# Block sums of a weight matrix and residual additions as accumulating transfers from GpSimd

## The chip, the cores and the metric

The kernel runs on one core of a Trainium2 chip. The metric is the device time of one execution in microseconds; lower is better. The engines are TensorE (PE, with its weight loads PEld), VectorE (DVE), ScalarE (ACT), GpSimd (POOL) and SyncE (SP), which issues the transfers.

## The reference

Two layers work on 256 tokens of width 1024. Each layer is a SwiGLU FFN (inner width 2816), a token mixer (a Mamba-2 branch and a gated DeltaNet branch), and a second FFN. The part that the change touches is the FFN:

```python
def swiglu(x, w_in, w_out):
    gate, up = jnp.split(x @ w_in, 2, axis=-1)
    return (jax.nn.silu(gate) * up) @ w_out

for l in range(DEPTH):
    h = h + 0.5 * swiglu(rms_norm(h, ffn1_norm[l]), ffn1_w_in[l], ffn1_w_out[l])
    ...   # the mixer adds to h
    h = h + 0.5 * swiglu(rms_norm(h, ffn2_norm[l]), ffn2_w_in[l], ffn2_w_out[l])
return rms_norm(h, final_norm)
```

All tensors are float32.

## The kernel before

Weights come from HBM in tiles of 128 x 1024 float32 (512 KB). Each form of a tile that TensorE uses is split into a high part (`whi`, a copy to float32r on ScalarE, line 67) and a low part (`wlo`, the difference on VectorE, line 70), and each product is three matmuls: high by high, low by high, high by low. A raw tile lives in a ring of NRAW = 5 buffers (`wraw`), and a split form in a ring of NSPL = 5 (`whi`, `wlo`). A load is issued by SP in order, and waits until the ring's oldest tile is done with, as a rule until its low part was computed.

An FFN of the kernel is written as a string, `FFN`: "f" is the first 256 inner channels, each "c" a chunk of 128 inner channels of gate and up (two weight tiles, 48 matmuls of 256 columns, into `fc`), and "A", "B", "d" are parts of the second product, `@ w_out`. The inner width is 22 blocks of 128. Six of them ("d") are multiplied directly. The other 16 are taken as eight pairs, two pairs to a group, so there are four groups in each of the four FFNs. For a pair the product is one of 2 x 2 blocks (two token halves, two inner blocks, two output halves) with seven block products in place of eight, each of sums of blocks. "A" runs four of the seven for a group of two pairs (into the PSUM tiles `p`), and "B" the other three (into `o`), after all chunks are done:

```python
FFN = "f" + 8 * "c" + "A" + 4 * "c" + "A" + 4 * "c" + "A" + 2 * "c" + "A" + 2 * "c" + "BdBBBddddd"
```

The sums of weight blocks are made on VectorE from the raw tiles of a group. `plan` lists the forms in the order of use, q0 to q3 for "A" and q4 to q6 for "B"; `prep` makes one form; `load` issues the load of one tile of `stream`; `take` hands a form to TensorE and keeps loads and forms ahead. The first tile of a group lies in a buffer of its own (`wfirst`, one of four slots that the mixer also uses), since its sum is kept from q0 to q6. Four sums a group are formed (`less`): three into `wfirst`, one into a `wraw` tile. Five tiles are loaded for a group: three at "A", and two at "B".

When all four "A" are done, `join` combines the four PSUM tiles with the factor 0.5 into the four quarters of the residual `h` (tiles `half`, `u2`, `u4`, `u5`; four additions to h). The products in `o` are added afterwards by `residual`, inside `norm_in`, where the next norm begins: square on ScalarE, `zz` on VectorE, the power -1/2 on GpSimd (`rsqrt`, line 190), the scaled rows `hn` on VectorE, and their transposes `hnT` on TensorE. The last part of an FFN, "ddddd", takes all five direct forms at once, for the first token half and then for the second.

The order on each engine comes from a scheduler that places an instruction when what it needs is there; a load whose buffer is free is put early. So the `wfirst` loads of an FFN stand on SP in the stage before it, where the slots come free.

Of the kernel before, what the change touches and what calls it, by code (L numbers as in the profile page):

```python
# [7 lines left out]
F32 = mybir.dt.float32  # L8
# [3 lines left out]
ALU = mybir.AluOpType  # L12
# [4 lines left out]
P = 128  # L17
# [6 lines left out]
FC = FF // 256  # L24
# [5 lines left out]
NRAW = 5  # L30
NSPL = 5
# [21 lines left out]
def trunk_kernel(ctx, tc, x, wst, wsm, norms, lpar, rpar, cst, out):  # L53
    nc = tc.nc
# [14 lines left out]
    def tt(o, a, b, op):  # L69
        return V.tensor_tensor(out=o, in0=a, in1=b, op=op)  # L70

    def stt(o, a, s, b, op0, op1):
        return V.scalar_tensor_tensor(out=o, in0=a, scalar=s, in1=b, op0=op0, op1=op1)  # L73
# [25 lines left out]

    def plan_plain(j, n):  # L100
        for i in range(j, j + n):
            stream.append(i)
            plan.append(("d", [len(stream) - 1], len(stream)))
        return j + n

    def plan_ffn(j):


        o, j2, held = j + 4 * FC, j + 4 * FC + 22, []
        for kind in FFN:  # L110
            if kind in "fc":
                j = plan_plain(j, 4 if kind == "f" else 2)
            elif kind == "d":
                o = plan_plain(o, 1)
            else:
                if kind == "A":
                    where = [len(stream) + i for i in range(3)]
                    stream.extend(range(o, o + 3))
                    held.append((where, o + 2))
                    o += 4  # L120
                    for i, need in enumerate((2, 3, 3, 3)):
                        plan.append((f"q{i}", where, where[0] + need))
                else:
                    where, b22 = held.pop(0)
                    where += [len(stream) + 1, len(stream)]
                    stream.extend([b22, b22 + 1])
                    for i in range(4, 7):
                        plan.append((f"q{i}", where, len(stream)))
        return j2

    j0 = 0
# [1 line left out]
        j0 = plan_ffn(plan_plain(plan_ffn(j0), mix))  # L133
    assert j0 == n_dram
    n_raw = len(stream)
    first = {js[0] for kind, js, _ in plan if kind == "q0"}
    n_forms = len(plan)
    state = {"loaded": 0, "prepped": 0, "taken": 0, "last": None, "hold": False, "behind": {}, "first": 0}
    raws, halves = {}, {}

    def load(j):
        if j in first:
            r = slots.tile([P, 1024], F32, tag=f"y{state['first']}", name="wfirst")
# [3 lines left out]
        state["last"] = nc.sync.dma_start(r[:], wst[stream[j] // 2, :, (stream[j] % 2) * 1024 :][:, 0:1024])  # L147
        raws[j] = r

    def prep(i):  # L150
        kind, js, _ = plan[i]
        hi = wpool.tile([P, 1024], F32R, tag="whi", name="whi", bufs=NSPL)
        lo = wpool.tile([P, 1024], F32R, tag="wlo", name="wlo", bufs=NSPL)

        def less(o, a, b):
            tt(raws[js[o]][:], raws[js[a]][:], raws[js[b]][:], ALU.subtract)


        r = raws[js[{"q2": 1, "q4": 4, "q5": 3}.get(kind, 0)]]
        with ExitStack() as behind:  # L160
            for ins in state["behind"].pop(i, ()):
                behind.enter_context(tc.issue_after(ins))
            act(hi[:], r[:])
            if kind == "q1":
                less(1, 2, 1)
            elif kind == "q2":
                less(0, 2, 0)
            elif kind == "q4":
                less(0, 3, 0)
            tt(lo[:], r[:], f(hi[:]), ALU.subtract)  # L170
            if kind == "q0":
                less(0, 1, 0)
        for o in {"d": (0,), "q2": (1,), "q3": (2,), "q4": (4,), "q5": (3,), "q6": (0,)}.get(kind, ()):
            raws.pop(js[o])
        halves[i] = (hi, lo)

    def ahead(key, n, fn):
        while state[key] < n:
            fn(state[key])
            state[key] += 1  # L180

    def take():
        j = state["taken"]
        state["taken"] = j + 1
        ahead("loaded", min(plan[min(j + NSPL, n_forms) - 1][2] + NRAW - 1, n_raw), load)
        ahead("prepped", min(j + 1 if state["hold"] else j + NSPL, n_forms), prep)
        return halves.pop(j)

# [204 lines left out]
    def join(pb):  # L393

        hv = [[h[:, t, n * 512 : (n + 1) * 512] for n in range(2)] for t in range(2)]
        half, u2, u4, u5 = (tmp2(n) for n in ("half", "u2", "u4", "u5"))
# [12 lines left out]
    def close_blocks(po, stat, sums, pb, nw):  # L409
# [24 lines left out]
    def ffn(nxt):  # L434
# [19 lines left out]
        def block_sums(p, g2):  # L454

            sf = tmp2("sf")
            a11, a21, a12, a22 = (g2[:, j * P : (j + 1) * P] for j in range(4))
            s1, s2_, s3, s4 = (sf[:, j * P : (j + 1) * P] for j in range(4))
            tt(s1, a21, a22, ALU.add)
            tt(s3, a11, a21, ALU.subtract)  # L460
            tt(s2_, s1, a11, ALU.subtract)
            tt(s4, a12, s2_, ALU.subtract)
# [27 lines left out]
        for c in range(FC - 1):  # L490
# [17 lines left out]
                block_sums(c + 1, g2)  # L508
            if todo[0] == "A":
                if not pb:  # L510
                    pb.update({i: trb(f"p{i}") for i in (1, 6, 5, 7)})
                four = [
                    (pb[1], lambda p: stat(2 * p, 0), PAIRS[n]),
                    (pb[5], lambda p: sums(p, 0), PAIRS[n]),
                    (pb[7], lambda p: sums(p, 2), PAIRS[n]),
                    (pb[6], lambda p: sums(p, 1), PAIRS[n]),
                ]
# [703 lines left out]
    for t in range(2):  # L1221
# [5 lines left out]
        r = rstd_of(t)  # L1227
# [137 lines left out]
```

## Time and profile before

| | |
|---|---|
| Median of 3 runs | 1567.72 us (1565.7 to 1568.12) |
| The profiled execution | 1568.61 us, span 1566.8 us |
| Granted TensorE clock | 0.999 |
| Transfers | 293.14 MB, mean 187 GB/s |
| `wraw` loads | 504 of 512 KB, 4.7 us from issue to landing |
| `wfirst` loads | 16 of 512 KB, 5.4 us from issue to landing |

A row of the profile's groups reads: line, engine, operation, written tile <- read tiles, shapes, count | busy us in total, mean ns of one | idle time of the engine just before, and what ended it. A row of waits reads: who waited, for whom, total us, times, longest us. A row of a timeline reads: start, duration, engine, line, operation, tiles, count, and in brackets the idle time before it. The share of the queue `q1` is the time that its packets took, of sixteen engines over the span.

### The profile page before, as it was taken

To read this page: it belongs to the slowest core of one execution; us is meant where nothing else is said; L and a number is where in the kernel's file an instruction comes from. 1 tells how busy PE (TensorE), PEld (TensorE's weight loads), DVE (VectorE), ACT (ScalarE), POOL (GpSimd) and SP (SyncE) were. 2 spreads that over 40 slices of the span, in tenths; PEclk is the share of its full clock that TensorE was granted. 3 is DMA by queue.
4 is the path that set the end of the run, shared out by engine and by line. 5 is a ranking of instruction groups with operands and counts; after the bars stand their busy time and mean duration, and the time that the engine had idled before them with its cause. 6 is when DMAs were issued, how large, how long until landed. Compare 5 with 4: busy or idle time off the path is not lost.

```text
span 1566.8 us, 28951 instructions
## 1 busy us (share of the span) xinstructions
PE 1535.5 (98%) x11452; PEld 1382.9 (88%) x11452; DVE 1252.7 (80%) x1888; ACT 949.7 (61%) x1534; POOL 53.7 (3%) x60
## 2 busy tenths in 40 slices
PE   8999999999999999999999999999999999999997
PEld 7999779999988888999799997899898888889995
DVE  6878869967899766878878887799589997677886
ACT  5656567766665545656555565676756665455554
POOL 0000010000000000000000002010000000000000
PEclk9999999999999999999999999999999999999999
DMA  8665565653565656565665557566445556556554
GB/s 294 215 203 178 197 215 175 179 160 113 177 215 162 193 198 196 170 212 188 229 215 189 174 186 223 182 190 188 116 136 202 175 178 209 192 179 192 170 185 134
DMA packets 94222, 293.14 MB, mean 187 GB/s; under 512 B 22325, under 2 KB 23301, under 8 KB 93062
## 3 DMA queue, kind: packets, MB, share of 16 engines
q1 hardware_dynamic: 94086, 291.29, 57.5%
q8 instruction: 90, 1.47, 0.4%
q14 instruction: 46, 0.38, 0.1%
HBM read 289.33 MB, written 1.92 MB: 186 GB/s over the span
## 4 chain that ended last, share of the span: by engine, by line
PE 67%; DVE 16%; DMA 6%; issue 5%; ACT 4%; POOL 1%; SPq 1%; POOLq 0%; ACTq 0%; DVEq 0%
PE fc L301 7%; PE fc L307 7%; DVE wlo L70 7%; PE fc L306 7%; DMA wraw<-in_wst_dram 5%; PE t L297 3%; PE t L296 3%; PE t L298 3%; PE b L298 3%; PE b L297 2%; PE b L296 2%; ACT whi L67 2%; DVE ca L73 1%; PE xs L301 1%; PE xs L306 1%
## 5 line engine op out<-in xcount | busy, mean ns | idle before, releaser
L70 DVE TENSOR_TENSOR wlo<-wraw,whi 128x1024 fp32r<-128x1024 f32 x488 | 591.3, 1220 | 173.2 <-ACT whi L67 165.2
L67 ACT ACTIVATE whi<-wraw 128x1024 fp32r<-128x1024 f32 x488 | 511.5, 1059 | 275.7 <-PE fc L306 85.5
L307 PE MATMUL fc<-uW,wlo 128*128 128x256 f32 x1280 | 354.7, 277 | 0.0
L301 PE MATMUL fc<-uW,whi 128*128 128x256 f32 x1280 | 354.0, 277 | 0.0
L306 PE MATMUL fc<-uW,whi 128*128 128x256 f32 x1260 | 348.1, 276 | 0.0
L301 PEld LDWEIGHTS fc<-uW,whi 128*128 128x128 f32 x1280 | 240.4, 188 | 0.8
L307 PEld LDWEIGHTS fc<-uW,wlo 128*128 128x128 f32 x1280 | 240.4, 188 | 0.0
L306 PEld LDWEIGHTS fc<-uW,whi 128*128 128x128 f32 x1260 | 236.5, 188 | 0.8
L67 ACT ACTIVATE whi<-wfirst 128x1024 fp32r<-128x1024 f32 x64 | 68.0, 1062 | 59.2 <-PE fc L306 34.0
L296 PE MATMUL t<-whi,uW 128*128 128x512 f32 x256 | 102.1, 400 | 0.0
L297 PE MATMUL t<-wlo,uW 128*128 128x512 f32 x256 | 100.8, 394 | 0.5 <-DVE wlo L70 0.5
L298 PE MATMUL t<-whi,uW 128*128 128x512 f32 x256 | 100.7, 394 | 0.0
L70 DVE TENSOR_TENSOR wlo<-wfirst,whi 128x1024 fp32r<-128x1024 f32 x64 | 78.0, 1218 | 6.8 <-ACT whi L67 5.9
L296 PE MATMUL b<-whi,bh 128*128 128x512 f32 x192 | 76.3, 399 | 0.0
L297 PE MATMUL o<-wlo,gh 128*128 128x512 f32 x160 | 65.4, 409 | 9.8 <-DVE wlo L70 9.6
L297 PE MATMUL b<-wlo,bh 128*128 128x512 f32 x192 | 74.9, 390 | 0.0
L298 PE MATMUL b<-whi,bl 128*128 128x512 f32 x192 | 74.3, 394 | 0.6 <-DVE bl L70 0.6
L70 DVE TENSOR_TENSOR wfirst<-wraw,wfirst 128x1024 f32<-128x1024 f32 x48 | 58.5, 1220 | 20.2 <-DMA wraw<-in_wst_dram 19.9
L301 PE MATMUL xs<-uW,whi 128*128 128x256 f32 x256 | 73.0, 285 | 0.0
L307 PE MATMUL xs<-uW,wlo 128*128 128x256 f32 x256 | 71.5, 279 | 0.0
L306 PE MATMUL xs<-uW,whi 128*128 128x256 f32 x256 | 71.3, 279 | 0.0
L298 PE MATMUL o<-whi,gl 128*128 128x512 f32 x160 | 62.6, 391 | 0.0
(319 smaller groups left out, 3401.3 us busy)
## 6 DMA issues: line engine op xcount, KB each, us to landing
wraw<-in_wst_dram SPq DMA_DIRECT2D x504, 512.0 KB, 4.7
wfirst<-in_wst_dram SPq DMA_DIRECT2D x16, 512.0 KB, 5.4
dc<-rdram SPq DMA_DIRECT2D x8, 1024.0 KB, 8.4
nw<-in_norms_dram SPq DMA_DIRECT2D x6, 512.0 KB, 6.1
gb<-rdram SPq DMA_DIRECT2D x8, 256.0 KB, 5.5
h<-in_x_dram SPq DMA_DIRECT2D x4, 256.0 KB, 5.5
out_dram<-fo SPq DMA_DIRECT2D x4, 256.0 KB, 2.0
dq<-X SPq DMA_DIRECT2D x2, 256.0 KB, 5.7
```

The source lines that it names most:

```text
L67: return A.activation(out=o, in_=i, func=func, **kw)
L70: return V.tensor_tensor(out=o, in0=a, in1=b, op=op)
L73: return V.scalar_tensor_tensor(out=o, in0=a, scalar=s, in1=b, op0=op0, op1=op1)
L296: PE.matmul(ps, lh, rh, start=start, stop=False)
L297: PE.matmul(ps, lh, rl, start=False, stop=False)
L298: return PE.matmul(ps, ll, rh, start=False, stop=stop)
L301: PE.matmul(ps, wh, mh, start=start, stop=False)
L306: PE.matmul(ps, wh, ml, start=False, stop=False)
L307: PE.matmul(ps, wl, mh, start=False, stop=stop)
```

## The change

Two of the four sums of a group are no longer computed on VectorE. The group's own tile, now named `wsum`, is loaded with the first block, and GpSimd issues a transfer that adds a second block from HBM to it (`"+"` in `stream`); after q3 another accumulating transfer adds the fourth block. The other two sums stay on VectorE, one during q1 and one during q0. The group's order is now q1, q0, q2, q3. The first block is loaded again as a plain tile for q0, and the second as one for the sum in q1, so a group has six plain loads and two accumulating ones, in place of five plain loads. The number of tiles that may be loaded ahead (`limit`) now counts ring tiles alone.

In `join` the four additions to `h` are now accumulating transfers from SBUF to SBUF, issued by GpSimd. Four operations on VectorE that make the `u` tiles remain. The first two products of "A" change places, and two signs in `block_sums` change.

```diff
@@ plan_ffn @@
+        for at, kind in enumerate(FFN):
+            if kind == "A":
+                spots.append(at - 2)
...
+            if at in spots:
+                y = len(stream)
+                stream.extend([("y", o1 + 4 * q), ("+", o1 + 4 * q + 1, y)])
+                begun.append(y)
+                q += 1
...
+            elif kind == "A":
+                y, u = begun.pop(0), len(stream)
+                stream.extend([("w", o + 1), ("w", o + 2), ("w", o)])
+                plan.append(("q1", (y, u, u + 1), u + 2))
+                plan.append(("q0", (u + 2, y, u + 1), u + 3))
+                plan.append(("q2", (u,), u + 3))
+                plan.append(("q3", (y, o + 3), u + 3))
+                held.append((y, o + 2))
+                o += 4
             else:
-                if kind == "A":
-                    where = [len(stream) + i for i in range(3)]
-                    stream.extend(range(o, o + 3))
...
+                y, b22 = held.pop(0)
+                stream.append(("w", b22))
+                plan.append(("q4", (len(stream) - 1,), len(stream)))
+                stream.append(("w", b22 + 1))
+                plan.append(("q5", (len(stream) - 1,), len(stream)))
+                plan.append(("q6", (y,), len(stream)))
@@ load, prep @@
+    def add_to(r, i):
+        G.dma_start(out=r[:], in_=tile_of(i), accum_op=ALU.add)
...
+        kind, i = stream[j][:2]
+        if kind == "+":
+            add_to(raws[stream[j][2]], i)
+            return
...
             act(hi[:], r[:])
-            if kind == "q1":
-                less(1, 2, 1)
-            elif kind == "q2":
-                less(0, 2, 0)
-            elif kind == "q4":
-                less(0, 3, 0)
+            if kind in ("q0", "q1"):
+                to, by = (raws[k][:] for k in js[1:])
+                tt(to, to, by, ALU.add)
             tt(lo[:], r[:], f(hi[:]), ALU.subtract)
-            if kind == "q0":
-                less(0, 1, 0)
...
+        if kind == "q3":
+            add_to(r, js[1])
@@ join @@
+        def onto(o, u):
+            G.dma_start(out=o, in_=u[:], accum_op=ALU.add)
+
         act(half[:], pb[1][:], scale=0.5)
-        stt(hv[0][0], pb[1][:], 0.5, hv[0][0], ALU.mult, ALU.add)
+        onto(hv[0][0], half)
         stt(u2[:], pb[6][:], 0.5, half[:], ALU.mult, ALU.add)
-        stt(u4[:], pb[5][:], 0.5, u2[:], ALU.mult, ALU.add)
-        tt(hv[0][1], hv[0][1], u4[:], ALU.add)
+        stt(u4[:], pb[5][:], 0.5, u2[:], ALU.mult, ALU.subtract)
+        onto(hv[0][1], u4)
         yield
-        stt(u2[:], pb[7][:], 0.5, u2[:], ALU.mult, ALU.add)
-        stt(u5[:], pb[5][:], 0.5, u2[:], ALU.mult, ALU.add)
-        tt(hv[1][0], hv[1][0], u2[:], ALU.add)
-        tt(hv[1][1], hv[1][1], u5[:], ALU.add)
+        stt(u3[:], pb[7][:], 0.5, u2[:], ALU.mult, ALU.add)
+        onto(hv[1][0], u3)
+        stt(u5[:], pb[5][:], 0.5, u3[:], ALU.mult, ALU.subtract)
+        onto(hv[1][1], u5)
```

How the order moves is shown at two places. The first is VectorE at the end of the first FFN, from the first low part of the third "B" to the last of the five direct tiles; `wfirst` and `wsum` are the group's sum, `u` the tiles of `join`. Before:

```order
L70 TENSOR_TENSOR wfirst<-wraw,wfirst 128x1024
L70 TENSOR_TENSOR wlo<-wraw,whi 128x1024
L70 TENSOR_TENSOR wlo<-wfirst,whi 128x1024
L70 TENSOR_TENSOR h<-h,u_1967 128x512
L70 TENSOR_TENSOR wlo<-wraw,whi 128x1024 x2
L73 SCALAR_TENSOR_TENSOR u_1966<-p_849,u_1966 128x512
L70 TENSOR_TENSOR wlo<-wfirst,whi 128x1024
L70 TENSOR_TENSOR wlo<-wraw,whi 128x1024 x2
L73 SCALAR_TENSOR_TENSOR u_1968<-p_848,u_1966 128x512
L70 TENSOR_TENSOR wlo<-wraw,whi 128x1024 x2
L70 TENSOR_TENSOR h<-h,u_1966 128x512
L70 TENSOR_TENSOR h<-h,u_1968 128x512
```

And of the changed kernel, from the third group's low parts to the first residual addition:

```order
L70 TENSOR_TENSOR wlo<-wsum,whi 128x1024
L70 TENSOR_TENSOR wlo<-wraw,whi 128x1024 x2
L70 TENSOR_TENSOR wlo<-wsum,whi 128x1024
L70 TENSOR_TENSOR wlo<-wraw,whi 128x1024 x5
L73 SCALAR_TENSOR_TENSOR h<-o,h 128x512 x2
```

The sums and the `u` tiles are gone from between the low parts; the four `u` tiles now stand together before the first direct tile.

The second place is GpSimd between the last power of the first mixer (`srr`) and the powers of the following two norms (`zz`). Before, nothing stands there:

```order
L753 TENSOR_TENSOR c_2305<-c_2305,pq 128x4
L190 TENSOR_TENSOR so_2309<-so,mhalf 128x4 x4
L190 TENSOR_TENSOR srr<-sss,mhalf 128x2 x4
L190 TENSOR_TENSOR zz<-zz,mhalf 128x1 x6
L660 MEMSET Q 128x2048
```

In the changed kernel:

```order
L212 TENSOR_TENSOR srr<-sss,mhalf 128x2 x4
L165 DMA wsum<-in_wst_dram 128x1024 x4
L212 TENSOR_TENSOR zz<-zz,mhalf 128x1 x2
L165 DMA wsum<-in_wst_dram 128x1024 x4
L421 DMA h<-half 128x512
L421 DMA h<-u_8631 128x512
L421 DMA h<-u_8632 128x512
L421 DMA h<-u_8633 128x512
L165 DMA wsum<-in_wst_dram 128x1024 x4
L212 TENSOR_TENSOR zz<-zz,mhalf 128x1 x2
```

The first accumulation of all four groups of an FFN now stands ahead of the norm that begins it, and in the second FFN of the first layer it stands behind that FFN's own four and the four transfers to `h`.

More of the change, by code (lines that the diff above doesn't have):

```diff
@@ L135, in trunk_kernel @@
     n_raw = len(stream)
-    first = {js[0] for kind, js, _ in plan if kind == "q0"}
+    limit = []
+    for _, _, need in plan:
+        m, room = need, NRAW
+        while m < n_raw:
+            room -= stream[m][0] == "w"
+            if not room:
+                break
+            m += 1
+        limit.append(m)
     n_forms = len(plan)
@@ L153, in prep @@
         lo = wpool.tile([P, 1024], F32R, tag="wlo", name="wlo", bufs=NSPL)
-        def less(o, a, b):
-            tt(raws[js[o]][:], raws[js[a]][:], raws[js[b]][:], ALU.subtract)
-        r = raws[js[{"q2": 1, "q4": 4, "q5": 3}.get(kind, 0)]]
+        r = raws[js[0]]
         with ExitStack() as behind:
@@ L184, in take @@
         state["taken"] = j + 1
-        ahead("loaded", min(plan[min(j + NSPL, n_forms) - 1][2] + NRAW - 1, n_raw), load)
+        ahead("loaded", limit[min(j + NSPL, n_forms) - 1], load)
         ahead("prepped", min(j + 1 if state["hold"] else j + NSPL, n_forms), prep)
```

40 lines of the change are left out of this document (17 added, 23 removed).

## The prediction

> **What bounds the kernel now.** I read the page first (busy times, DMA queue, chain of waits), then the waits of TensorE, then the windows over the ends of the four FFNs, then the timelines of VectorE and ScalarE there.
>
> ```profile
> span 1566.8 us, 28951 instructions
> PE 1535.5 (98%) x11452; PEld 1382.9 (88%) x11452; DVE 1252.7 (80%) x1888; ACT 949.7 (61%) x1534; POOL 53.7 (3%) x60
> q1 hardware_dynamic: 94086, 291.29, 57.5%
> PEld o L297 <- DVE wlo L70: 21.6, 32, 1.8
> PE o L297 <- DVE wlo L70: 9.6, 16, 1.4
> ```
>
> TensorE is busy 98% of the span, so 31.3 us (1566.8 - 1535.5) is all that shows as idle, and nothing in the change makes TensorE's own work shorter. The one idle group that VectorE causes is "o <- wlo": the output products at the end of an FFN, which wait for the low half of a weight tile; 9.6 us on TensorE's matmul side, 21.6 on the weight-load side. These two rows are bounds, since a matmul's end is modelled. To get nearer I count matmuls. The first two and last two rows of one group of products give the pace, and the windows give the count:
>
> ```profile
> 123.86 0.39 PE L296 MATMUL p<-whi,gh 128*128 128x512 f32 x1
> ...
> 129.09 0.39 PE L298 MATMUL p<-whi,bsa 128*128 128x512 f32 x1
> 161.00:184.00 23.00, 21.47 (x89) 15.75 (x88) 21.41 (x24) 13.15 (x13) 0.00 (x0) 1.00 0.72 237
> 753.00:777.00 24.00, 21.85 (x89) 16.15 (x90) 21.78 (x23) 13.22 (x14) 0.00 (x0) 1.00 0.86 303
> 936.00:959.00 23.00, 21.56 (x89) 15.91 (x88) 21.13 (x22) 13.24 (x14) 0.00 (x0) 1.00 0.76 241
> 1529.00:1552.00 23.00, 20.26 (x83) 14.84 (x82) 20.19 (x22) 11.96 (x12) 0.00 (x0) 1.00 0.54 176
> ```
>
> There are 23 steps from 123.86 to 129.09, so a 512-wide matmul leaves every 0.227 us although its row says 0.39. In the windows the columns are length, busy PE with its count, PEld, DVE, ACT, POOL, granted clock, DMA share, GB/s. 89 matmuls take 20.2 us at that pace, so the four ends lose 2.8, 3.8, 2.8 and 4.1 us (23 - 83 x 0.227), 13.5 us together; if the fourth lacks six records as against the others, 12. VectorE is busy 84.5 of the 93 us. **About 12 us is the prize**; it is 0.8% of the span.
>
> What is late there, in the first FFN:
>
> ```profile
> 176.38 1.06 ACT L67 ACTIVATE whi<-wraw 128x1024 fp32r<-128x1024 f32 x1 [1.27 <-DMA wraw<-in_wst_dram]
> 178.48 1.06 ACT L67 ACTIVATE whi<-wraw 128x1024 fp32r<-128x1024 f32 x1 [1.04 <-DMA wraw<-in_wst_dram]
> 178.19 2.34 DVE L70 TENSOR_TENSOR wlo<-wraw,whi 128x1024 fp32r<-128x1024 f32 x2
> 180.46 1.28 DVE L70 TENSOR_TENSOR h<-h,u 128x512 f32<-128x512 f32 x2
> 181.66 1.21 DVE L70 TENSOR_TENSOR wlo<-wraw,whi 128x1024 fp32r<-128x1024 f32 x1
> ```
>
> Two residual additions (1.28 us) stand ahead of the last low half, and the two tiles before it waited for their loads. A load waits for one of five buffers, and a buffer is freed by a low half on VectorE: late VectorE makes late loads.
>
> **The change part by part.** Removed from VectorE:
>
> ```profile
> L70 DVE TENSOR_TENSOR wfirst<-wraw,wfirst 128x1024 f32<-128x1024 f32 x48 | 58.5, 1220 | 20.2 <-DMA wraw<-in_wst_dram 19.9
> L70 DVE TENSOR_TENSOR wraw<-wraw 128x1024 f32<-128x1024 f32 x16 | 19.5, 1218 | 0.1
> L70 DVE TENSOR_TENSOR h<-h,u 128x512 f32<-128x512 f32 x12 | 7.9, 681 | 0.0
> L73 DVE SCALAR_TENSOR_TENSOR h<-p,h 128x512 f32<-128x512 f32 x4 | 2.7, 682 | 0.0
> ```
>
> Of 64 sums (48 + 16), 32 stay: 32 x 1.22 = 39.0 us go. All 16 additions to h go, 7.9 + 2.7 = 10.6 us. Together 49.6 us, 12.4 per FFN. Most lies beside a TensorE that never waits (the whole "A" part), and is worth nothing. On the path are, in each end, the four additions for q4 (4 x 1.22 = 4.9 us) and the four to h (2.7 us): 7.6 us off an engine with about 2 us of idle time in 23. That is more than the 2.8 to 4.1 us lost, so VectorE is no longer last there.
>
> What is next: the fifth tile of the last five needs the buffer of the product just before it. High half 1.06 and low half 1.21 us make 2.3 us, and TensorE asks for it after four tiles of three matmuls, 12 x 0.227 = 2.7 us. That fits by 0.4 us, so I give back a quarter: **-6.5 us** of 8.3 to 9.7 in the first, third and fourth end (bounds -10 and 0).
>
> Added: per group of blocks one more plain load (6 for 5), two accumulating loads of 512 KB; per FFN four accumulating transfers of 256 KB from SBUF. SP issues 16 more loads; each queues behind a buffer as before. In the "A" part three tiles instead of two take ring buffers, yet the slot tile no longer counts against the ring, and four tiles' matmuls (10.9 us) lie between a buffer's release and its next use; I cost it at nothing, and 1 us per group, 16 us, if loads took twice as long. ScalarE's high halves stay as many.
>
> No accumulating transfer is in the trace. The nearest rows:
>
> ```profile
> wraw<-in_wst_dram SPq DMA_DIRECT2D x504, 512.0 KB, 4.7
> dq<-X SPq DMA_DIRECT2D x2, 256.0 KB, 5.7
> 28.00:48.00 20.00, 20.00 (x179) 20.00 (x178) 12.40 (x19) 10.60 (x15) 0.00 (x0) 1.00 0.94 323
> 48.00:60.00 12.00, 12.00 (x108) 12.00 (x108) 8.92 (x15) 6.95 (x11) 0.00 (x0) 1.00 0.61 186
> ```
>
> 57.5% of 1566.8 us moved 291.29 MB, so 512 KB (0.524 MB) occupies all sixteen engines 1.6 us: the lower bound of an accumulating one. The dq row as a duration, 5.7 us for 256 KB, makes 11.4 us: the upper bound. I take 3.2 us, twice a plain load, nearer the first row since tile shape and source are its own, and twice since old contents must be fetched as well. Engine time added: 16 x 1.6 + 32 x 3.2 + 16 x 1.6 = 154 us, which lifts the share from 57.5 to 67%: room on average. Not so in two places. At 28 to 48 us the engines are 94% busy; four accumulations (12.8 us) fall there, with 1.2 + 4.7 us free until 60 and a lead of five tiles of 2.7 us: **+0.5 us** (0 to 5). In the second end, 753 to 777 at 86%, four loads for the next FFN already run; four accumulations behind them and four to h bring 12.8 + 6.4 = 19 us into 24 us with 3.4 us free. Loads there land later by about 3 us with a lead of four tiles of 1.36 us: what VectorE gives back is lost again, **-0.5 us** (-4 to +8).
>
> In the other ends the transfers to h are 6.4 us of engine time against 28% of 23 us, 6.4, free (46% in the fourth): they fit. Their results are wanted late: the u tiles are now all made right after the gating product of the last chunk (156.28 in the trace), the first residual read was at 183.69:
>
> ```profile
> 183.69 0.69 DVE L73 SCALAR_TENSOR_TENSOR h<-o,h 128x512 f32<-128x512 f32 x1 [0.82 <-PE o L298]
> 156.28 0.41 DVE L70 TENSOR_TENSOR g<-sg,fc 128x256 f32<-128x256 f32 x1
> 780.56 0.55 POOL L190 TENSOR_TENSOR zz<-zz,mhalf 128x1 f32<-128x1 f32 x1 [174.24 <-DVE zz L78]
> 767.71 0.33 SPq L147 DMA_DIRECT2D wfirst<-in_wst_dram  x1
> DMA to landing us min/median/max: 5.4/5.5/5.7
> 465.68 2.20 POOL L190 TENSOR_TENSOR srr<-sss,mhalf 128x2 f32<-128x2 f32 x1 [25.64 <-DVE sss L78]
> ```
>
> 27 us cover four transfers; without cover the norm would wait, us for us. GpSimd gets waits in its queue: at the second end four accumulations stand ahead of the norm's power (zz), the last one waiting for a load issued at 767.71 and landing 5.5 us later, 773.2. An issue on GpSimd has no row; its longest operation there, 2.2 us, as bound gives 775.4, and zz ran at 780.56. 5 us of cover, cost nothing; if lost, VectorE's hn and then TensorE's transposes wait behind it.
>
> The Trainium skill speaks against the change: "DMA: Bandwidth & Descriptors", section "Issuing engines are not separate DMA queues", says that GpSimd's transfers run on the same sixteen engines and interleave with SP's, and "Rules for kernel authors" there says that an accumulate reads its destination and writes it later. By these the work is moved onto an engine set that is 86 to 94% busy in two places, as in my terms above; taken as a separate queue the two terms would be 0 and -3.
>
> **Sum.** -6.5 - 0.5 + 0.5 = -6.5 us. The profiled execution took 1568.61 us (span 1566.8 and 1.8 around it), 0.9 above the median 1567.72. 1568.6 - 6.5 = 1562.1; against the median 1561.2. I predict **1561.5 us**.
>
> **The rivals.** *Full gain.* All four ends recover: -12 and something of the stall at the second end's beginning, 1555 us. For it: VectorE's surplus is twice the loss. Against: 0.4 us of margin at the fifth tile. *Nothing moves.* The loads are what is late (the 1.27 and 1.04 us above), and contention keeps them so: 1567 us. For it: the DMA share of 0.72 to 0.86 in three of the ends. Against: the fourth end has 0.54 and loses as much, so VectorE is late by itself. *Slower: accumulations hold the engines.* Place: the start (28 to 48 us) and the second end. It decides from about 5 us of engine time each (four are 20 us, the start has 5.9 free and 13.6 of lead). At 6.5 us, between my bounds: start 26 - 19.5 = +6.5; second end 26 + 13 = 39 against 3.4 free, 5.4 of lead, half of it falling behind the end, +15; the others' transfers to h, 13 against 6.4 + 5.4, +1.2 each; less the 8 that VectorE gives: 1568.6 + 6.5 + 15 + 3.6 - 8 = 1586, and by the same sum 1575 at 5.5 us. For it: nothing in the trace shows an accumulation's price. Against: landing of plain loads is 4.7 us with 1.6 of engine time. *The change does not do what it says* only if GpSimd's order lets an accumulation delay zz: a share of the slower case.
>
> **How the numbers follow.** Forecast (1558 to 1565) 0.46, full gain 0.14, nothing 0.16, slower 0.24. The range 1554 to 1577 leaves out the far part of the slow case and a little below the full gain. A measurement here tells about 0.2%, 3.1 us. Faster takes most of the forecast and the full gain, 0.46 x 0.95 + 0.14 + a little of the nothing case = 0.60; same 0.14; slower 0.26.
>
> **What would show it.** Right: idle of "o <- wlo" on the weight-load side from 21.6 to under 10 us; VectorE about 50 us less busy; matmul counts of the ends as before in windows 2 us shorter; DMA share 63 to 67%. Wrong: TensorE or ScalarE waiting for wraw loads where there was none (20 to 60 us, the second end), an accumulation's landing far above 6 us, or VectorE's h waiting for a transfer.

## The result and the profile after

The changed kernel takes 1559.53 us (median of 5 runs, 1558.51 to 1561.29) against 1567.72 us for the kernel before (5 runs on the same chip). The ratio is 0.9949, 95% interval 0.9938 to 0.9961: 8 us less, beyond the 0.2% that a measurement can tell. The forecast was 1561.5 us. The profiled execution took 1561.29 us, so the traces compare 1559.5 us of span with 1566.8.

From the page of the changed kernel, the span, the busy times and the two DMA queues:

```profile
span 1559.5 us, 29036 instructions
PE 1533.0 (98%) x11452; PEld 1387.0 (89%) x11452; DVE 1209.6 (78%) x1840; ACT 945.0 (61%) x1534; POOL 95.9 (6%) x108
q1 hardware_dynamic: 96390, 299.68, 57.0%
q0 software_dynamic: 6912, 20.97, 7.8%
```

VectorE is 43.1 us less busy (1252.7 before), and a second queue has appeared, that of GpSimd's transfers. Both queues together take 64.8% of the engines.

The waits of TensorE at the output products, from the list of waits:

```profile
PEld o L319 <- DVE wlo L70: 3.6, 5, 1.1
PEld o L318 <- ACT whi L67: 2.8, 2, 1.8
PE o L319 <- DVE wlo L70: 1.6, 4, 0.8
```

The group "o <- wlo" fell from 21.6 to 3.6 us on the weight-load side and from 9.6 to 1.6 us on the matmul side. The windows over the four FFN ends, same columns as in the prediction:

```profile
160.00:183.00 23.00, 22.58 (x98) 18.05 (x97) 20.59 (x21) 14.26 (x16) 2.67 (x3) 1.00 0.98 298
751.00:775.00 24.00, 20.89 (x84) 15.84 (x83) 15.18 (x14) 12.06 (x12) 2.60 (x3) 0.93 1.05 325
934.00:957.00 23.00, 23.00 (x104) 19.03 (x103) 18.19 (x17) 15.04 (x16) 0.04 (x1) 1.00 0.87 267
1521.00:1545.00 24.00, 24.00 (x107) 19.85 (x106) 19.21 (x19) 14.95 (x16) 0.57 (x1) 1.00 0.67 204
```

The third and fourth windows are full: TensorE never stops. The second is worse than before (20.89 busy of 24, where it was 21.85), its clock was granted at 0.93 on average, and the DMA share there is 1.05.

To compare many kernels I used one more count on each trace. For every matmul I took the distance to the next one's start and subtracted the median distance of matmuls of its width; summed from the first to the last output product of an FFN, that is the time lost in that end. "Start" is the same sum over the first 130 us. The losses belong to one traced execution of each kernel, the time is the median of all of its runs, and the ratio is taken to runs of the kernel before in the same session (medians 1567.28 to 1569.38 us). All in us:

| kernel | start | end 1 | end 2 | end 3 | end 4 | four ends | median time | ratio to before, 95% interval |
|---|---|---|---|---|---|---|---|---|
| before | 8.8 | 3.3 | 5.6 | 3.4 | 5.2 | 17.5 | 1567.72 | 1 |
| changed | 11.0 | 1.0 | 7.1 | 0.0 | 0.0 | 8.1 | 1559.53 | 0.9949 (0.9938 to 0.9961) |
| changed, h additions on VectorE | 10.0 | 1.1 | 5.9 | 0.2 | 0.2 | 7.4 | 1558.94 | 0.9951 (0.9938 to 0.9963) |
| before, h additions as transfers | 10.7 | 3.4 | 9.1 | 5.6 | 7.5 | 25.6 | 1571.67 | 1.0027 (1.0017 to 1.0038) |
| changed, next FFN's loads held | 10.6 | 0.0 | 0.0 | 0.0 | 0.0 | 0.0 | 1550.91 | 0.9903 (0.9890 to 0.9916) |
| the same, h additions on VectorE | 10.4 | 1.5 | 0.0 | 0.2 | 0.3 | 2.0 | 1555.26 | 0.9920 (0.9901 to 0.9938) |
| before, next FFN's loads held | 9.4 | 3.9 | 4.2 | 3.4 | 4.4 | 15.9 | 1567.71 | 0.9996 (0.9986 to 1.0007) |
| changed, transfers without addition | 11.0 | 0.0 | 2.6 | 0.0 | 0.0 | 2.6 | 1557.37 | 0.9931 (0.9914 to 0.9948) |
| before, sums on 8 columns | 9.7 | 0.3 | 5.2 | 2.0 | 1.6 | 9.1 | 1559.32 | 0.9954 (0.9940 to 0.9969) |
| before, q4's sum later, loads held | 8.8 | 0.2 | 0.2 | 0.2 | 1.1 | 1.7 | 1552.70 | 0.9898 (0.9884 to 0.9913) |
| before, q4's sum later | 9.8 | 0.2 | 0.2 | 0.1 | 0.6 | 1.1 | 1553.00 | 0.9904 (0.9889 to 0.9919) |
| the same, held, sums on 8 columns | 9.6 | 0.0 | 0.0 | 0.0 | 0.0 | 0.0 | 1552.00 | 0.9888 (0.9872 to 0.9903) |
| changed, a wait put back | 9.7 | 6.4 | 13.2 | 5.8 | 2.7 | 28.1 | 1578.84 | 1.0071 (1.0056 to 1.0086) |
| changed, each block transfer twice | 14.8 | 1.4 | 28.1 | 1.9 | 0.3 | 31.7 | 1588.40 | 1.0134 (1.0111 to 1.0156) |

From before to changed the ends give 9.4 us and the start takes 2.2 of it in this pair: 7.2 of the 7.3 us of span. The start varies by itself: over the table it is 9.5 us on average in the seven kernels without a block transfer from GpSimd (8.8 to 10.7) and 10.5 in the six with one for each sum (9.7 to 11.0). Most of the 2.2 us can't come from the transfers: 1.2 us of it is lost before 20 us, where the windows from 14 to 18 us have 22 matmuls in the kernel before and 12 in the changed one, and GpSimd issues its first accumulation only later:

```profile
36.87 1.03 POOL L165 DMA_DIRECT2D wsum<-in_wst_dram  x1 [20.88 <-PE fc L329]
```

From 20 to 130 us the seven kernels lose 0.4 us on average and the six 0.7.

Two traced executions lie well above their kernel's median, so the losses of these rows are larger than in a median run: 1577.23 us against 1571.67 for "before, h additions as transfers", and 1597.39 against 1588.40 for "changed, each block transfer twice".

### The profile page after: what moved, and what is told of

It is laid out like the page before. It is cut to its first block, busy times and chain, and to the rows that moved or that the text cites. A ratio compares the mean times of both kernels' runs of the same rounds, so it can differ in the third digit from the quotient of the medians.

```text
span 1559.5 us, 29036 instructions
## 1 busy us (share of the span) xinstructions
PE 1533.0 (98%) x11452; PEld 1387.0 (89%) x11452; DVE 1209.6 (78%) x1840; ACT 945.0 (61%) x1534; POOL 95.9 (6%) x108
## 4 chain that ended last, share of the span: by engine, by line
PE 83%; DVE 7%; DMA 3%; issue 3%; ACT 3%; POOL 1%; SPq 0%; POOLq 0%; ACTq 0%; DVEq 0%
PE fc L329 9%; PE fc L323 9%; PE fc L328 9%; DVE wlo L70 3%; PE t L319 3%; PE t L318 3%; PE t L320 3%; PE b L320 3%; PE b L319 3%; PE b L318 2%; PE o L320 2%; PE o L319 2%; PE o L318 2%; DMA wraw<-in_wst_dram 2%; PE p L319 2%
## 5 line engine op out<-in xcount | busy, mean ns | idle before, releaser
L70 DVE TENSOR_TENSOR wlo<-wraw,whi 128x1024 fp32r<-128x1024 f32 x504 | 611.1, 1221 | 174.5 <-ACT whi L67 166.9
L67 ACT ACTIVATE whi<-wraw 128x1024 fp32r<-128x1024 f32 x504 | 527.1, 1058 | 273.9 <-PE fc L328 87.7
L70 DVE TENSOR_TENSOR wlo<-wsum,whi 128x1024 fp32r<-128x1024 f32 x48 | 58.6, 1221 | 14.7 <-ACT whi L67 13.8
L67 ACT ACTIVATE whi<-wsum 128x1024 fp32r<-128x1024 f32 x48 | 50.8, 1058 | 28.4 <-PE fc L328 23.8
L318 PE MATMUL o<-whi,gh 128*128 128x512 f32 x160 | 63.8, 399 | 1.9 <-ACT whi L67 1.9
L165 POOL DMA_DIRECT2D wsum<-in_wst_dram x32 | 28.1, 878 | 584.3 <-DVE wlo L70 455.1
```

Of the source, the lines that this page charges most:

```text
L67: return A.activation(out=o, in_=i, func=func, **kw)
L165: G.dma_start(out=r[:], in_=tile_of(i), accum_op=ALU.add)
L318: PE.matmul(ps, lh, rh, start=start, stop=False)
```

## The experiments

### The two halves of the change, each alone

First, the sums by transfer alone: in the changed kernel the additions to `h` go back to VectorE.

```diff
-        onto(hv[0][0], half)
+        stt(hv[0][0], pb[1][:], 0.5, hv[0][0], ALU.mult, ALU.add)
...
-        onto(hv[1][1], u5)
+        tt(hv[1][1], hv[1][1], u5[:], ALU.add)
```

> Only the block sums go by accumulating transfers; the four additions to h of each FFN are back on VectorE. Theory (VectorE was late at the ends of the FFNs, and the change pays by the operations it takes from there): two additions to h stand again ahead of the last low half, about 1.2 us lost in each of three ends, while the second end has 1 MB less to accumulate and gains up to 2: 1561 us (1559 to 1564). Rival (the sums alone matter, the additions to h cost nothing there): as the changed kernel or a little faster, 1557 to 1559.5.

Measured: 1558.94 us, the same as the whole change and in the rival's range, not the theory's. The additions to `h`, which the prediction counted with 2.7 us an end, bring nothing.

Second, the other half alone: the kernel before, with its additions to `h` as accumulating transfers and nothing else.

```diff
-        stt(hv[0][0], pb[1][:], 0.5, hv[0][0], ALU.mult, ALU.add)
+        onto(hv[0][0], half)
...
-        tt(hv[1][1], hv[1][1], u5[:], ALU.add)
+        onto(hv[1][1], u5)
```

> Only the additions to h go by accumulating transfers; all four block sums are back on VectorE, and the loads are those of the kernel before. Theory: the sums are the larger part of the relief (4.9 of 7.6 us in an end), so less than half of the gain: 1564 us (1562 to 1566.5). Rival (the additions to h, which stand right ahead of the last low half, are what is late): nearly all of the gain, 1559 to 1561.

Measured: 1571.67 us, ratio 1.0027: slower, against both theories. Taking 10.6 us of work from VectorE made the ends of the traced execution lose 8 us more; the medians are 4.4 us apart (1567.28 in that session). From its waits and its queues:

```profile
ACT whi L67 <- DMA wraw<-in_wst_dram: 28.2, 14, 4.5
q0 software_dynamic: 2304, 4.20, 1.7%
```

ScalarE waited 28.2 us for weight loads, 19.7 in the kernel before. The transfers are only 1.7% of the engines' time, but they fall into the ends. This was a first hint that what is late there is the loads, and something that passes their lateness on. It is a weak one: ScalarE waits 50.4 us for weight loads in the changed kernel, which is faster. Why this kernel is slower was not tried further; about 4.4 of the 8 us are 22 matmuls at half clock, at the price of the last section.

### The second end: what the accumulations meet

In the changed kernel's second end the chain is short. Two rows of TensorE's timeline, with the idle time ahead of them and what ended it:

```profile
769.04 0.50 PE L318 MATMUL o<-whi,gh 128*128 128x512 f32 x1 [0.55 <-ACT whi L67]
772.37 0.79 PE L318 MATMUL o<-whi,gh 128*128 128x512 f32 x1 [1.34 <-ACT whi L67]
```

TensorE waits for high halves. ScalarE's timeline at the same place:

```profile
771.26 1.06 ACT L67 ACTIVATE whi<-wraw 128x1024 fp32r<-128x1024 f32 x1 [2.28 <-DMA wraw<-in_wst_dram]
```

ScalarE waits 2.28 us for a load. The DMA issues between 740 and 790 us in the changed kernel, with the median time from issue to landing at the end:

```profile
wraw<-in_wst_dram SPq DMA_DIRECT2D x16, 512.0 KB, 8.8
wsum<-in_wst_dram POOLq DMA_DIRECT2D x4, 512.0 KB, 8.9
```

And in the kernel before, in the same stretch:

```profile
wraw<-in_wst_dram SPq DMA_DIRECT2D x18, 512.0 KB, 5.3
wfirst<-in_wst_dram SPq DMA_DIRECT2D x4, 512.0 KB, 5.5
```

The loads land after 8.8 us instead of 5.3. The first loads and the accumulations of the next FFN run in the middle of it, as the scheduler puts them as early as buffers allow. The next experiment holds those first loads of the second layer's first FFN behind the loads queued before them:

```diff
+        with ExitStack() as after:
+            if kind == "y" and state["tail"] is not None:
+                after.enter_context(tc.issue_after(state["tail"].ins))
             state["last"] = nc.sync.dma_start(r[:], tile_of(i))
```

> The changed kernel, but the first loads of the four sums of the second layer's first FFN are issued behind the loads that are already queued when the FFN before it ends, so that neither they nor the accumulations behind them fall into that end. Theory (loads for the next FFN and their accumulations make the second end wait for its own weights): the 7 us that this end still loses go, the half clock there too, 1553 us (1551 to 1556). Rival (the transfers to h and the end's own loads are enough to fill the transfer engines): 1557 to 1560.

Measured: 1550.91 us, as the theory had it (0.1 us below its range). The second end of this kernel, from its windows:

```profile
752.00:775.00 23.00, 23.00 (x103) 19.03 (x103) 15.29 (x15) 13.37 (x16) 0.56 (x1) 1.00 0.77 261
```

Its loads between 740 and 790 us:

```profile
wraw<-in_wst_dram SPq DMA_DIRECT2D x18, 512.0 KB, 5.3
```

TensorE is busy all the time, the DMA share is 0.77 instead of 1.05, and a load lands after 5.3 us again. The cost of the transfers in this kernel was that collision, 7.1 us, and an order of the loads avoids it. With the additions to `h` on VectorE as well:

> The hold, the block sums by accumulating transfers, and the additions to h on VectorE. Theory (after the hold the transfers to h fit beside the loads, and VectorE's two late additions cost 0.4 to 1.2 us an end): 1553 us (1551 to 1555), slower than with the transfers to h. Rival (the transfers to h disturb the loads of the ends more than they relieve VectorE, as where they were made alone): 1548 to 1550.

Measured: 1555.26 us, 0.3 us above the theory's range and far from the rival's. The intervals of the two (0.9890 to 0.9916 and 0.9901 to 0.9938) overlap, so whether the transfers to `h` are worth something once the loads are held stays open. Holding the same loads in the kernel before:

> The kernel before, with the same hold: the group tiles of the second layer's first FFN are loaded only after the FFN ahead of it has ended; no transfer is added. Theory (VectorE is late by itself in every end, and in the second one loads come on top): the second end falls to the 3 us of the first and third, 1565 us (1563.5 to 1566.5). Rival (these loads alone make the second end slow, and holding them is worth as much as in the changed kernel, where it gave 8.6 us): 1559 us.

Measured: 1567.71 us, no change, which neither the theory nor the rival had. In the kernel before something else was last, even in the second end.

### What an addition in a transfer costs

Line 165 is issued 32 times as before, but without `accum_op`:

```diff
-        G.dma_start(out=r[:], in_=tile_of(i), accum_op=ALU.add)
+        G.dma_start(out=r[:], in_=tile_of(i))
```

> The changed kernel, with the 32 accumulating loads of blocks issued by GpSimd as plain loads into the same tiles: the addition is left out, issue and bytes from HBM stay. Theory (an accumulation costs the transfer engines twice a plain load, and this fills the second end): the software queue's share falls from 7.8% to about 4.8%, the second end loses 2 to 4 us less, 1556.5 us (1554.5 to 1558.5). Rival (the loads and their order are the cost, not the addition): 1558.5 to 1560.

Measured: 1557.37 us, inside the theory's range, and its software queue:

```profile
q0 software_dynamic: 6912, 20.97, 5.0%
```

The same packets and bytes take 5.0% of 1557.8 us in place of 7.8% of 1559.5: 43.7 us less of all engines for 32 tiles, 1.4 us a tile. In the packets' records a 4 KB packet of these loads has a median of 159 ns without addition and 328 ns with it, 2.06 times, and all of them together make 3.0 us of engine time for an accumulated tile. The second end then loses 2.6 us in place of 7.1.

Doubled, the same cost: each accumulation is issued twice.

```diff
+        for _ in range(2):
+            G.dma_start(out=r[:], in_=tile_of(i), accum_op=ALU.add)
```

> The changed kernel with each of the 32 accumulating block transfers issued twice, so that a block is added twice. It doubles what the accumulations take of the engines: at the 3.0 us of engine time for one that the software queue's 7.8% gave, some 97 us more, a share of about 14% for that queue. Theory A (the accumulations cost by the engine time they hold at the start and at the second end, 4 x 3.0 = 12 us more at each place): start and second end lose together 4 to 9 us more, 1564 to 1569 us. The slow rival of the prediction, with its sum at 6.0 us for one tile (1575 at 5.5, 1586 at 6.5): 1580 us. Theory C (they cost by the order in which loads are started alone): 1559 to 1562 us.

Measured: 1588.40 us, slower than the kernel before by 1.34%, and more than any of the three had. Its software queue, from the page:

```profile
q0 software_dynamic: 11520, 37.75, 13.1%
```

13.1% of 1595.6 us less 7.8% of 1559.5 is 87 us, 2.7 us for one more accumulation: the price of one did not rise. What rose is a wait. GpSimd's timeline at the second end, with its idle time in brackets:

```profile
798.45 1.75 POOL L166 DMA_DIRECT2D wsum<-in_wst_dram  x2 [10.06 <-DMA wsum<-in_wst_dram]
807.29 0.86 POOL L166 DMA_DIRECT2D wsum<-in_wst_dram  x1 [7.09 <-DMA wsum<-in_wst_dram]
807.86 0.88 POOL L213 TENSOR_TENSOR zz<-zz,mhalf 128x1 f32<-128x1 f32 x1
```

GpSimd's queue stands still, 10.06 and 7.09 us: the second accumulation into a tile waits until the first one has landed, and the norm's power `zz` stands behind them. So doubling brought a wait that the changed kernel doesn't have there, and this run is no clean test of the engine time alone. The waits between 760 and 812 us say who waits for that:

```profile
DVE hn L73 <- POOL zz L213: 13.8, 1, 13.8
PE hnT L285 <- DVE hn L73: 12.3, 1, 12.3
```

VectorE's `hn` waits 13.8 us for `zz`, and TensorE's transposes 12.3 us for `hn`. A window of 6 us in this stretch:

```profile
799.00:805.00 6.00, 0.00 (x0) 0.00 (x0) 0.00 (x0) 0.00 (x0) 1.20 (x2) 0.67 0.82 138
```

There is not one matmul in it. Of the 31.7 us lost in the ends, 28.1 are in this one.

### Amount of work, or a wait

In the kernel before, q4's preparation puts the fourth sum (`less(0, 3, 0)`, which needs the group's other "B" tile) ahead of q4's own low half. VectorE at the second end of the kernel before, from its timeline:

```profile
757.21 1.21 DVE L70 TENSOR_TENSOR wlo<-wraw,whi 128x1024 fp32r<-128x1024 f32 x1
759.59 1.22 DVE L70 TENSOR_TENSOR wfirst<-wraw,wfirst 128x1024 f32<-128x1024 f32 x1 [1.16 <-DMA wraw<-in_wst_dram]
760.73 1.22 DVE L70 TENSOR_TENSOR wlo<-wraw,whi 128x1024 fp32r<-128x1024 f32 x1
```

VectorE stands idle for 1.16 us until the other tile has landed, then computes the sum, and only then the low half of a tile that TensorE needs first. The longest such wait stands where this end begins:

```profile
744.24 1.23 DVE L70 TENSOR_TENSOR wfirst<-wraw,wfirst 128x1024 f32<-128x1024 f32 x1 [4.29 <-DMA wraw<-in_wst_dram]
```

The list of waits has 19.9 us in 11 places of this kind, all at the four ends; the group's row in the prediction shows the same at its end. To separate this wait from the work, the first kernel keeps every wait and makes the operations small: all 64 sums and the 16 additions to `h` on 8 columns.

```diff
-            tt(raws[js[o]][:], raws[js[a]][:], raws[js[b]][:], ALU.subtract)
+            tt(raws[js[o]][:, 0:8], raws[js[a]][:, 0:8], raws[js[b]][:, 0:8], ALU.subtract)
```

> The kernel before, with the block sums and the additions to h done on 8 columns instead of 1024 and 512, so that most of both is left out: VectorE's relief alone, without any added transfer. Theory: all that VectorE's lateness cost goes, and the price of the transfers isn't paid: 1554 us (1551 to 1557), the second end keeping some wait for its loads. Rival (the changed order of forms, and the sum's tile no longer counting against the ring, bring the gain): 1563 to 1568.

Measured: 1559.32 us, between the theory's range and the rival's, and as fast as the changed kernel. VectorE is 1185.4 us busy, 67 less than before, where the change took 43; the ends lose 9.1 us in place of 17.5. So less work gives back half of the loss, and half stays. From its list of waits:

```profile
DVE wfirst L70 <- DMA wraw<-in_wst_dram: 27.2, 11, 4.9
PEld o L297 <- DVE wlo L70: 8.1, 11, 1.5
```

The wait for the load grew to 27.2 us: a faster VectorE only arrives earlier at it. The opposite kernel removes no work and only turns the order, on VectorE alone:

```diff
-            elif kind == "q4":
-                less(0, 3, 0)
-            tt(lo[:], r[:], f(hi[:]), ALU.subtract)
+            low = tt(lo[:], r[:], f(hi[:]), ALU.subtract)
...
+            elif kind == "q4":
+                with tc.issue_after(low.ins):
+                    less(0, 3, 0)
```

It ran first together with the held loads, then by itself.

> The kernel before with the hold, and with the sum that goes with q4 moved behind q4's low half on VectorE: before, that sum needs the second tile of a B, so that the first tile's low half waited for the second tile's load. No work is removed and no transfer added. Theory (part of the gain of the change is this lost wait, 19.9 us of idle VectorE before the sums): 1560 us (1557 to 1563). Rival (only less work on VectorE helps): as with the hold alone, 1563.5 to 1566.5.

> The kernel before with one change: on VectorE the sum for q4 stands behind q4's low half instead of ahead of it. No work is removed, nothing is transferred differently, and the loads of the next FFN are not held back. Theory A (the low half of q4 waited for the load of the group's other "B" tile, and the loads of the next FFN are a second cost that shows only once this wait is gone): the first, third and fourth ends recover to about 1 us lost each, the second keeps 4 us or more; 1558 to 1561 us. Rival B (this wait was the whole loss, and holding the loads adds nothing to it): 1551 to 1554 us. Rival C (only the two together matter, as each lets the other late load through): 1565 us or more.

Measured: 1552.70 and 1553.00 us. Both theories of the first expectation were too high, and the second kernel fell to its rival B: the order was the whole loss, and holding the loads adds nothing. From the page of the kernel that only turns the order, VectorE's busy time and the group of its sums:

```profile
PE 1528.5 (99%) x11452; PEld 1383.2 (89%) x11452; DVE 1253.6 (81%) x1888; ACT 946.8 (61%) x1534; POOL 53.7 (3%) x60
L70 DVE TENSOR_TENSOR wfirst<-wraw,wfirst 128x1024 f32<-128x1024 f32 x48 | 58.6, 1220 | 0.1
```

VectorE does all of its work, 1253.6 us, 48 sums of 1.22 us among it, and idles 0.1 us in front of them instead of 20.2. The wait of TensorE for a low half at the ends, from the list of waits:

```profile
PE o L298 <- DVE wlo L70: 0.2, 1, 0.2
```

It was 9.6 us. ScalarE's waits for weight loads fell too, from 19.7 to 10.9 us; that fits a low half which runs earlier and so frees its buffer earlier. The windows over the first two ends:

```profile
160.00:183.00 23.00, 23.00 (x102) 18.81 (x101) 21.81 (x22) 12.45 (x14) 0.00 (x0) 1.00 0.67 207
750.00:774.00 24.00, 24.00 (x107) 19.66 (x106) 20.87 (x24) 14.90 (x18) 0.55 (x1) 1.00 0.86 291
```

In the first end VectorE is busy 21.81 of 23 us, a little more than before (21.41), and TensorE loses nothing. A VectorE that is 95% busy was not what was late.

If that holds, less work should bring nothing once the order is right:

> The kernel before with q4's sum behind q4's low half, with the first loads of the second FFN of layer 1's successor held behind the queued ones, and with all 64 sums and all 16 additions to h cut down to 8 of their columns: that part of the computation is left out, about 85 us of VectorE's work. Theory A (what was late was the wait, not the amount of VectorE's work): as with the same two edits and the full work, 1551 to 1553 us. Theory B (VectorE's amount of work still costs something): 1549 us or less.

Measured: 1552.00 us, as theory A had it; its interval (0.9872 to 0.9903) overlaps those of the two kernels above. And the wait alone, put into the changed kernel, should lose what the change had won:

The edit also counts that tile among those that q4 needs, as the kernel before does.

```diff
-                plan.append(("q4", (len(stream) - 1,), len(stream)))
+                plan.append(("q4", (len(stream) - 1, len(stream)), len(stream) + 1))
...
+            if kind == "q4":
+                few = small([P, 8], "few")
+                b = raws[js[1]][:, 0:8]
+                behind.enter_context(tc.issue_after(tt(few[:], b, b, ALU.subtract).ins))
             tt(lo[:], r[:], f(hi[:]), ALU.subtract)
```

> The changed kernel with one operation more per group: a subtraction on 8 columns of the group's second "B" tile on VectorE, placed ahead of q4's low half. It puts back the wait for that tile's load and next to no work (16 operations, well under 0.2 us each). Theory A (the change gains since q4's low half no longer waits for the second tile's load): the ends lose 2 to 4 us each again, 1564 to 1569 us, the time of the kernel before. Theory B (the change gains since VectorE has 7.6 us less to do in an end): the ends stay as in the changed kernel, 1559 to 1561 us.

Measured: 1578.84 us, on the side of theory A and 10 us past its range, slower than the kernel before. From its list of waits:

```profile
DVE few L70 <- DMA wraw<-in_wst_dram: 37.9, 16, 4.7
PEld o L323 <- DVE wlo L70: 20.1, 15, 3.4
```

16 operations of 0.17 us wait 37.9 us for their loads, against 19.9 us in the kernel before. "o <- wlo" is back at 20.1 us although VectorE has 1208.7 us to do, as in the changed kernel. It puts back more waiting than the kernel before had, so it shows that the wait is enough to lose everything, not what exactly it cost there. The traces show two parts of the surplus. In the four ends a weight load lands after 5.7, 8.7, 5.5 and 5.7 us, in the changed kernel after 5.0, 8.8, 5.0 and 7.0, in the kernel before after 4.1, 5.3, 4.7 and 4.9 (windows 150 to 190, 740 to 790, 925 to 975 and 1510 to 1565 us). And three stretches of these ends ran at half clock, which no end of the kernel before did; windows cut to them:

```profile
165.70:169.10 3.40, 3.40 (x9) 2.64 (x8) 3.40 (x5) 3.07 (x4) 0.00 (x0) 0.50 1.01 237
780.10:786.90 6.80, 5.80 (x12) 3.76 (x13) 3.14 (x3) 1.89 (x4) 0.86 (x1) 0.50 1.04 337
967.80:971.20 3.40, 3.13 (x7) 2.48 (x8) 0.90 (x2) 0.72 (x2) 0.00 (x0) 0.50 0.87 271
```

The windows have 28 matmuls. At half clock a 512-wide one leaves every 0.427 us in place of 0.227 (last section), so these make about 5.6 us of the 10.6 by which the ends lose more than in the kernel before.

## Why the prediction was right, and where its reason was not

**The place and the size of the prize: right, a little small.** The four ends lose 17.5 us by starts of matmuls in the kernel before; the windows gave 12 to 13.5, since they were cut inside the ends. The idle of "o <- wlo" went under 10 us as said, to 3.6, and the DMA share to 64.8%, inside 63 to 67.

**"VectorE is late by itself": the step that failed.** The prediction read 84.5 busy us of 93 as the cause, and took 7.6 us of operations in each end as the relief. With all operations kept and one of them moved behind another, the ends lose 1.1 us in place of 17.5. What was late was the low half of q4, held behind a sum that waited for another tile's load. The change wins since it takes this sum out of the end altogether, which the prediction listed only as 1.22 us of work. Its own row said so: 19.9 us of idle time ahead of these sums, which the prediction shows and does not use. Less work does help where the wait stays (1559.32 us with next to none of it, as much as the change won); that VectorE then catches up behind the wait is the likely reason. Without the wait, less work is worth nothing that shows (1552.00 against 1552.70 us). So VectorE's work mattered, for about half of the loss, only while that wait stood ahead of it.

**The first, third and fourth end, -6.5 us (bounds -10 and 0): -10.9 by starts.** These ends went from 3.3, 3.4 and 5.2 to 1.0, 0 and 0 us. Of the quarter that the prediction gave back for the fifth direct tile, about 2 us, 0.5 us was lost at that tile, in the first end alone; the other 0.5 us of that end was lost at 162.3 us, before the direct tiles.

**The second end, -0.5 us (bounds -4 and +8): +1.5.** Reason and place were right: loads of the next FFN and accumulations behind them make the direct tiles' loads late, 8.8 us from issue to landing. The sign of being wrong that was named for this place came true: between 740 and 790 us ScalarE waited 6.5 us for `wraw` loads, 2.2 in the kernel before. The Trainium skill's rule that the prediction weighed ("DMA: Bandwidth & Descriptors", "Issuing engines are not separate DMA queues") says that SP's and GpSimd's transfers share their engines; the trace agrees, with 5.3 us that became 8.8. With the loads held the ends lose nothing. The "full gain" rival, 1555 us, was too high for what can be had: three kernels reach 1551 to 1553.

**The loads of "A", cost at nothing: right.** The sums for q1 wait 37.2 us for them on VectorE, in 16 places, but the ends and the start make up 7.2 of the 7.3 us by which the span changed, so no loss of that kind is left for the "A" parts.

**The price of an accumulation, 3.2 us of engine time: 3.0 in the trace**, and 1.4 us more than the same load without addition. For another reducing transfer, the ReduceScatter step of a ring of ranks, the Trainium skill has a reason in "Collectives: The Full Stack", section "The bandwidth ceiling: the fold count and why AG ≠ RS ≠ AR": it is slower since the add needs two source reads, not since adding takes time. The 2.06 of the packets would fit that; no run here shows the reason. Its landing, from the DMA issues of the changed kernel, and its issue on GpSimd, from the groups:

```profile
wraw<-in_wst_dram SPq DMA_DIRECT2D x520, 512.0 KB, 5.0
wsum<-in_wst_dram POOLq DMA_DIRECT2D x32, 512.0 KB, 7.3
h<-u POOLq DMA_DIRECT2D x12, 256.0 KB, 6.8
L165 POOL DMA_DIRECT2D wsum<-in_wst_dram x32 | 28.1, 878 | 584.3 <-DVE wlo L70 455.1
```

It lands after 7.3 us, somewhat above the 6 us that the prediction named as a limit, and takes 0.88 us to issue, under the 2.2 us taken as bound. The start, +0.5 us (bounds 0 and +5), came out at 0.3 after 20 us (0.4 and 0.7 us above), less than the spread of either group of kernels.

**GpSimd's queue, 5 us of cover: right.** From its timeline in the changed kernel:

```profile
775.20 0.86 POOL L165 DMA_DIRECT2D wsum<-in_wst_dram  x1 [7.22 <-DMA wsum<-in_wst_dram]
781.98 0.56 POOL L212 TENSOR_TENSOR zz<-zz,mhalf 128x1 f32<-128x1 f32 x1 [5.91 <-DVE zz L78]
```

The last accumulation is issued by 776.06, and `zz` waits 5.91 us for VectorE. The prediction said what follows if that cover is lost, and the doubled kernel, with its added wait in that queue, shows it at the same place, 12.3 us on TensorE.

**The transfers to `h`: the cover was right, the gain was not.** No wait of VectorE for them shows, but their removal from VectorE brought nothing, and alone they cost 0.27%; whether they help once the loads are held stays open. They fell under the same wrong step: work removed from an engine that was not late by its work.

**The slow rival** asked for 5 us or more of engine time each, and the trace has 3.0. At double load its sign was right, by the queue on GpSimd more than by the engines.

**The sum** came out within 2 us since errors cancelled: the three ends gave 4.4 us more than taken, the second took 2.0 us more, and the start 1.7 more in this pair of traces, 1.2 of it ahead of the first transfer. With the cause taken wrong as well, that closeness is in good part luck. VectorE's 49.6 us were 43.1 in the busy time. Rows of 1.22 us start 1.14 us after one another (759.59 and 760.73 above), so their sum overstates it: without the overlap 46.0 us of sums and additions went, and the operations that remain, overlapping less, came to 3 us more.

## What to carry to other kernels

An engine that is 90% busy ahead of a stall is not thereby the cause: look in its idle time for what it waited, and whether the operation behind that wait was the one needed. Here one sum in each group, moved behind one low half, gave 0.96% without any transfer, more than the change's 0.51%. Where transfers from another engine are added, ask first what stands behind them in that engine's queue and which loads they meet, and hold back the loads that are early for no reason.

## What the hardware showed that was not expected

A few short waits of TensorE can cost more than their length. In the second end of the changed kernel, windows of 3 us:

```profile
769.00:772.00 3.00, 1.24 (x3) 0.48 (x3) 1.23 (x1) 0.73 (x1) 0.00 (x0) 0.96 1.06 287
772.00:775.00 3.00, 2.16 (x4) 1.45 (x5) 1.33 (x2) 0.32 (x1) 0.00 (x0) 0.50 1.03 265
775.00:778.00 3.00, 3.00 (x8) 2.31 (x7) 0.58 (x1) 0.72 (x2) 0.86 (x1) 0.50 1.02 406
```

After 3 us in which TensorE was busy for 1.24, the granted clock is 0.50, and still is while TensorE is busy without a gap; 8 matmuls run in 3 us, where a full end has 13 or 14. Eight of its matmuls start between 775.08 and 778.07 us, one every 0.427 us. The Trainium skill, "TensorE: Matmul & The Clock Gate", section "What's actually happening", gives half rate after at least one idle window of about 3.4 us. Here three matmuls ran in the 3 us ahead of it, and no wait in the timeline rows of its matmuls above is longer than 1.34 us. The same shows in the second end of the changed kernel with its additions to `h` on VectorE, where the longest wait was 1.71 us:

```profile
770.30:773.70 3.40, 1.61 (x6) 1.13 (x7) 1.58 (x2) 0.97 (x1) 0.00 (x0) 1.00 1.04 272
773.70:777.10 3.40, 3.40 (x10) 2.65 (x9) 0.34 (x1) 0.72 (x2) 0.86 (x1) 0.50 1.02 405
```

So in these two ends waits that were spread over a few microseconds were enough. In the changed kernel the half clock lasted 6.83 us, in which 13 matmuls started; at 0.427 us in place of 0.227 each, that makes 2.6 of the 7.1 us lost in this end, on top of the waits themselves.
